# Latent attention: the queries' rotation done in the PSUM bank of their product, and both parts of all 96 rows made from it in one instruction each

## The chip, the cores and the metric

One core of a Trainium2 chip runs the whole program. The metric is the device time of one execution in microseconds, taken as the median of three runs. A profiled execution gives the rows shown below; L1561 is line 1561 of the kernel's file.

The engines are called PE or TensorE (matrix products), PEld (its weight loads), DVE or VectorE, ACT or ScalarE, POOL or GpSimd, and SP, which issues the DMAs. SBUF is the large on-chip memory, PSUM the one that TensorE writes to; PSUM has banks of 128 partitions by 512 fp32 columns. POOL's operands in this kernel are all in SBUF.

## The reference, cut to what matters

Two layers of a trunk over 256 context and 512 latent tokens. In each, a gated DeltaNet group and a latent attention group stand side by side, between two feed-forward parts. The attention has 8 heads with 64 plain dimensions and 32 rotated ones:

```python
q = (rmsnorm(c_q, q_norm) @ w_uq).reshape(B, T, 8, 64 + 32)
q_nope, q_rope = q[..., :64], q[..., 64:]
# latent tokens alone are rotated: x1*cos - x2*sin, x2*cos + x1*sin
q_rope = concatenate([q_rope[:, :L], rope2d(q_rope[:, L:], cos, sin)])
qf = concatenate([q_nope, q_rope], axis=-1)
kf = concatenate([k_nope, broadcast(k_rope)], axis=-1)
s = einsum('bqhd,bkhd->bhqk', qf, kf) * MLA_SCALE
p = softmax(s); o = einsum('bhqk,bkhd->bqhd', p, v)
```

Latent queries read all 768 keys, context queries the 256 of the context. In the second layer only latent queries are needed.

## The kernel before

Everything is kept with the channels on the partitions and the tokens along the columns. An fp32 operand is split into a high part (`h`, cast to fp32r) and the rest (`l`, the difference), and a product is made of three: high by high, high by low, low by high. So wherever a new operand arises, ScalarE makes the high part and VectorE or POOL subtracts it to make the low part.

`mla` does the attention of one layer, head by head. `prep(h)` lists what a head needs before its scores, in pieces:

- `q_proj` makes the queries' product in a PSUM bank named `qps` (9 matmuls of 512 columns for the latent tokens, 9 of 256 for the context). The weight columns are laid out so that rows 0 to 63 of the bank are the plain dimensions, 64 to 95 the rotated ones, and 96 to 127 the same with their halves exchanged. The table `tab` holds the cosines in rows 64 to 95 and the signed sines in rows 96 to 127, so a rotation is two products and a sum.
- `p_lat` makes `qh` and `ql`, the two parts of the latent queries: rows 0 to 63 plain, 64 to 95 rotated. This is the piece that the change edits. `p_ctx` does the same for the context's queries without a rotation, in the first layer alone.
- `p_keys` makes the keys' parts: for an even head from two products (`kps`), for an odd head from a copy `kp`.
- `p_max1` and `p_max2` multiply the high parts alone (`smx`, `smc`) and reduce each row's maximum on VectorE; `p_neg` and `p_row` turn it into one more row (row 96) of the queries, `rp`, so that the scores come out less the maximum.

Then come the scores of that head, `score` (`sT`: three matmuls of 512 columns for each tile of 128 keys, two exponentials on ScalarE to `ph` and to `pf` or `sum`, a difference `pl` at L1645 and a running sum at L1648), and three steps later `weigh` (`po`), and at a head's end the division (`dn`, `rb`, `oT`, L1670 to L1689). The pieces of head h+1 are dealt out among the score steps of head h. For heads 0 and 1 the pieces run ahead of all scores, and in the first of them the DeltaNet group's output norm (`out_norm`, L1398 to L1413, and L1424, L1425) still runs on the same engines.

PSUM's eight banks are divided for the attention: three (`mm0`) for `sT`, `vps`, `dn`, `rb`, `rp`; three (`mm1`) for `qps`, `smx`, `smc`, `kps`; two for `po` and others. A bank is given out again when all that use it are done. `qr` is a buffer of 128 by 1024 from the ring of four that the raw weights use too.

The order on each engine is not that of the text: a planner walks through the program with its own estimates of each instruction's time and of the priorities (`hp` raises one) and writes each engine's queue before the run. On the chip each queue runs strictly in that order and waits by semaphores.

Of the kernel before, what the change touches and what calls it, by code (L numbers as in the profile page):

```python
# [5 lines left out]
F32 = mybir.dt.float32  # L6
# [3 lines left out]
ALU = mybir.AluOpType  # L10
# [4 lines left out]
P = 128  # L15
NL = 512
# [18 lines left out]
class K:  # L35
# [1394 lines left out]
    def p3(self, ps, wh, wl, xs, kt, off, n, cnt):  # L1430
        nc = self.nc
        xh, xl = xs
        nc.tensor.matmul(ps, wh, xh[:, off : off + n], start=kt == 0, stop=False)
        nc.tensor.matmul(ps, wh, xl[:, off : off + n], start=False, stop=False)
        nc.tensor.matmul(ps, wl, xh[:, off : off + n], start=False, stop=kt == cnt - 1)
# [35 lines left out]
    def mla(self, l, last):  # L1471
        nc, d = self.nc, self.d
# [43 lines left out]
        n64, r32 = slice(0, 64), slice(64, 96)  # L1516

        def keys(pr):
            kh, kl = kb[0]
            kp = ap.tile([P, NT], F32, tag="kp", name="kp", bufs=1)  # L1520
            for off, n in ((0, NL), (NL, NC)):
                ps = self.kvp.pop(("k", pr, off), None) or self.k_prod(pr, off, n)
                c = slice(off, off + n)
                nc.scalar.copy(kh[n64, c], ps[n64])
                nc.vector.tensor_sub(kl[n64, c], ps[n64], kh[n64, c].bitcast(F32))
                nc.scalar.copy(kp[n64, c], ps[64:128])
            kpo[pr] = kp

        def prep(h):

            pr, odd = h // 2, h % 2
            kh, kl = kb[odd]
            qh, ql = qb[odd]
            mx = ap.tile([P, 8], F32, tag="mx", name="mx", bufs=2)
            m2 = ap.tile([P, 8], F32, tag="m2", name="m2", bufs=2)

            def q_proj(off, n):
                ps = self.bank("qps")[:, :n]
                for kt in range(3):
                    cs = slice((odd * 3 + kt) * P, (odd * 3 + kt + 1) * P)  # L1540
                    p3(ps, wq[pr][0][:, cs], wq[pr][1][:, cs], cq[kt], kt, off, n, 3)
                return ps

            def p_keys():
                if odd:
                    kp = kpo[pr]
                    (nc.scalar.copy if 0 else nc.vector.tensor_copy)(kh[n64, :], kp[n64, :])
                    (nc.vector if 0 else nc.gpsimd).tensor_sub(kl[n64, :], kp[n64, :], kh[n64, :].bitcast(F32))
                    if pr < 3:
                        wq[pr + 1] = self.load_w(d["uq"][l, pr + 1], 768)  # L1550
                else:
                    keys(pr)

            def p_lat():
                ps = q_proj(0, NL)
                c = slice(0, NL)
                t = self.wp.tile([P, 1024], F32, tag="raw", name="qr", bufs=4)
                u, w = t[:, 0:NL], t[:, NL : 2 * NL]
                nc.scalar.copy(u, ps)
                nc.scalar.copy(qh[n64, c], u[n64])  # L1560
                nc.vector.tensor_tensor(out=w[r32], in0=u[r32], in1=self.tab[r32], op=ALU.mult)  # L1561
                nc.vector.tensor_tensor(out=u[r32], in0=u[96:128], in1=self.tab[96:128], op=ALU.mult)  # L1562
                (nc.vector if 0 else nc.gpsimd).tensor_sub(ql[n64, c], u[n64], qh[n64, c].bitcast(F32))
                (nc.vector if 1 else nc.gpsimd).tensor_add(w[r32], w[r32], u[r32])
                nc.scalar.copy(qh[r32, c], w[r32])
                (nc.vector if 1 else nc.gpsimd).tensor_sub(ql[r32, c], w[r32], qh[r32, c].bitcast(F32))

            def p_ctx():
                if last:
                    return  # L1570
                ps = q_proj(NL, NC)
                c = slice(NL, NT)
                nc.scalar.copy(qh[0:96, c], ps[0:96])
                nc.vector.tensor_sub(ql[0:96, c], ps[0:96], qh[0:96, c].bitcast(F32))

            def p_max1(t):
                ps = self.bank("smx")
                nc.tensor.matmul(ps, qh[0:96, t * P : (t + 1) * P], kh[0:96, 0:NL], start=True, stop=True)
                nc.vector.reduce_max(mx[:, t : t + 1], ps, axis=AX)  # L1579

            def p_max2(t2):
                ps = self.bank("smc")
                for j in range(2):
                    t = 2 * t2 + j
                    nc.tensor.matmul(ps[:, j * 256 : (j + 1) * 256], qh[0:96, t * P : (t + 1) * P], kh[0:96, NL:NT], start=True, stop=True)
                nc.vector.reduce_max(m2[:, 2 * t2 : 2 * t2 + 2], ps.rearrange("p (a c) -> p a c", a=2), axis=AX)

            def p_neg():
                nc.vector.tensor_max(m2[:, 0:4], m2[:, 0:4], mx[:, 0:4])
                nc.vector.tensor_scalar(out=m2[:, :ntq], in0=m2[:, :ntq], scalar1=-1.0, scalar2=None, op0=ALU.mult)  # L1590

            def p_row():
                for g0, g1 in ((0, 4), (4, ntq)):
                    if g0 == g1:
                        continue
                    rp = self.bank("rp")
                    for t in range(g0, g1):
                        nc.tensor.matmul(rp[96:128, (t - g0) * P : (t - g0 + 1) * P], m2[:, t : t + 1].to_broadcast([P, 32]), self.ident, start=True, stop=True)
                    nc.scalar.copy(qh[96:97, g0 * P : g1 * P], rp[96:97, : (g1 - g0) * P])

            f = {}
            def at(i, p, *a, hi=0):
                def go():
                    with self.hp(hi and h > 0):
                        p(*a)
                f.setdefault(i, []).append(go)

            T = 91102222220 if last else 90112222333
            T = [int(c) for c in str(T)[1:]]
            if h < 2:  # L1610
                T = [1, 0, 2] + [3] * 7
            at(T[0], p_lat, hi=0)
            at(T[1], p_keys, hi=0)
            if not last:
                at(T[2], p_ctx, hi=0)
            for t in range(4):
                at(T[3 + t], p_max1, t, hi=1)
            for t in range(2 if last else 3):
                at(T[7 + t], p_max2, t, hi=1)
            at(max(T[3:10]), p_neg, hi=1)  # L1620
            at(6 if h < 2 else 5 if last else 6, p_row, hi=0)
            return [lambda i=i: [p() for p in f.get(i, [])] for i in range(8)]
# [78 lines left out]
        ps = prep(0)  # L1701
# [316 lines left out]
```

## Time and profile before

| | |
|---|---|
| median of 3 runs | 3298.61 us (3295.17 to 3299.12) |
| the profiled execution | 3296.14 us, span 3294.4 us |
| TensorE, VectorE, ScalarE, POOL busy | 93%, 77%, 42%, 39% of the span |
| granted clock of TensorE, mean | 0.953 of full speed |
| attention of the first layer | about 980 to 1155 us |
| attention of the second layer | about 2700 to 2870 us |

Busy shares are those of the whole span; the two attention stages take about a tenth of it. The span is the time from the first to the last instruction; the execution's own time is 1.7 us longer. An instruction's time in the profile includes what it waits inside the engine once it has started.

### The profile page before, as it was taken

The page shows a single profiled execution, that of the slowest core. Times are in us where ns is not written, and L with a number is a line of the kernel's source. Part 1 is how long each engine was busy: PE and PEld are TensorE (multiplying, and loading weights), DVE is VectorE, ACT ScalarE, POOL GpSimd, SP SyncE. Part 2 cuts the span into 40 slices and gives each one's busy share as a digit, 9 for nine tenths or more (in the row PEclk, how much of TensorE's full clock was granted, in tenths as well). Part 3 has the DMA queues.
Part 4 walks back from the last instruction along what each step waited for, and adds up shares of the span by engine and source line. Part 5 has one row for each costly group of instructions (what it writes and reads, how often), then busy time and mean ns, then how long its engine had stood idle before and what let it go on. Part 6 is the DMA issues. An engine that isn't in the chain of part 4 may idle for free. (4 is left out here: it accounts for less than half of the span.)

```text
span 3294.4 us, 53696 instructions
## 1 busy us (share of the span) xinstructions
PE 3056.4 (93%) x20836; PEld 2785.1 (85%) x20836; DVE 2550.1 (77%) x4369; ACT 1376.2 (42%) x2600; POOL 1298.7 (39%) x1028
## 2 busy tenths in 40 slices
PE   7999999889899999999999899999989788989998
PEld 4899989878787789899999898899877676789998
DVE  7788887777778958777777987677777879777777
ACT  4333223544445645322335432223454346554343
POOL 5222122544656664222215321221554546744233
PEclk8999999889998899999999899999989899999999
DMA  6333333221310122323324343332322310224333
GB/s 223 109 122 128 99 128 119 90 74 52 100 64 11 39 90 77 123 90 103 103 71 135 103 141 111 116 127 90 115 82 65 89 46 9 93 77 154 97 109 97
DMA packets 149815, 318.68 MB, mean 97 GB/s; under 512 B 38184, under 2 KB 79528, under 8 KB 149560
## 3 DMA queue, kind: packets, MB, share of 16 engines
q1 hardware_dynamic: 149560, 315.25, 29.4%
q8 instruction: 163, 2.67, 0.3%
q14 instruction: 92, 0.75, 0.1%
HBM read 285.17 MB, written 30.03 MB: 96 GB/s over the span
## 5 line engine op out<-in xcount | busy, mean ns | idle before, releaser
L94 POOL TENSOR_TENSOR wlo<-wraw,whi 128x1024 fp32r<-128x1024 f32 (+1 forms) x228 | 589.6, 2596 | 1396.5 <-ACT whi L93 1357.5
L93 ACT CAST whi<-wraw 128x1024 fp32r<-128x1024 f32 (+2 forms) x482 | 469.4, 978 | 712.5 <-PE ps L778 344.8
L519 PE MATMUL ps<-zh,whi 128*128 128x256 f32 (+1 forms) x1208 | 386.1, 328 | 8.8 <-ACT zh L472 8.8
L609 PE MATMUL ps<-zl,whi 128*128 128x384 f32 (+1 forms) x1216 | 391.8, 322 | 0.0
L608 PE MATMUL ps<-zh,whi 128*128 128x384 f32 (+1 forms) x1216 | 391.6, 322 | 0.1
L610 PE MATMUL ps<-zh,wlo 128*128 128x384 f32 (+1 forms) x1216 | 390.3, 321 | 0.0
L520 PE MATMUL ps<-zl,whi 128*128 128x256 f32 (+1 forms) x1208 | 378.6, 324 | 5.7 <-DVE zl L477 5.7
L777 PE MATMUL ps<-gh,whi 128*128 128x512 f32 (+1 forms) x1008 | 350.6, 356 | 17.7 <-ACT gh L618 16.7
L778 PE MATMUL ps<-gl,whi 128*128 128x512 f32 (+1 forms) x1008 | 341.4, 354 | 25.4 <-DVE gl L619 25.4
L522 PE MATMUL ps<-zh,wlo 128*128 128x256 f32 (+1 forms) x1208 | 350.1, 323 | 0.1
L94 DVE TENSOR_TENSOR wlo<-wraw,whi 128x1024 fp32r<-128x1024 f32 (+1 forms) x254 | 295.3, 1163 | 24.8 <-ACT whi L93 23.4
L780 PE MATMUL ps<-gh,wlo 128*128 128x512 f32 (+1 forms) x1008 | 297.9, 350 | 0.0
L519 PEld LDWEIGHTS ps<-zh,whi 128*128 128x128 f32 x1208 | 234.5, 198 | 38.5 <-ACT zh L472 11.2
L520 PEld LDWEIGHTS ps<-zl,whi 128*128 128x128 f32 x1208 | 236.4, 196 | 24.2 <-DVE zl L477 6.6
L777 PEld LDWEIGHTS ps<-gh,whi 128*128 128x128 f32 x1008 | 193.4, 194 | 61.8 <-ACT gh L618 19.5
L778 PEld LDWEIGHTS ps<-gl,whi 128*128 128x128 f32 x1008 | 194.6, 193 | 54.9 <-DVE gl L619 27.9
L243 DVE CUSTOM_DVE_ANT_0 abraw<-abraw,srow 128x1024 f32<-128x1024 f32 x128 | 210.2, 1642 | 32.1 <-DMA abraw<-in_wat 29.9
L608 PEld LDWEIGHTS ps<-zh,whi 128*128 128x128 f32 x1216 | 229.4, 189 | 1.8 <-ACT whi L93 0.5
L609 PEld LDWEIGHTS ps<-zl,whi 128*128 128x128 f32 x1216 | 229.5, 189 | 0.4
L610 PEld LDWEIGHTS ps<-zh,wlo 128*128 128x128 f32 x1216 | 229.0, 188 | 0.0
L522 PEld LDWEIGHTS ps<-zh,wlo 128*128 128x128 f32 x1208 | 221.0, 197 | 6.9 <-issue 0.7
L608 PE MATMUL ps<-t42h,whi 128*128 128x384 f32 (+1 forms) x608 | 197.3, 324 | 7.6 <-ACT whi L93 7.6
(394 smaller groups left out, 7615.2 us busy)
## 6 DMA issues: line engine op xcount, KB each, us to landing
wraw<-in_wu SPq DMA_DIRECT2D x176, 512.0 KB, 3.3
abraw<-in_wat SPq DMA_DIRECT2D x128, 512.0 KB, 3.4
wraw<-in_wd SPq DMA_DIRECT2D x88, 512.0 KB, 3.5
wraw<-in_wi SPq DMA_DIRECT2D x44, 512.0 KB, 3.4
wraw<-in_wo SPq DMA_DIRECT2D x16, 512.0 KB, 3.8
xs<-x SPq DMA_DIRECT2D x64, 128.0 KB, 1.7
x<-xs SPq DMA_DIRECT2D x64, 128.0 KB, 3.3
x<-in_x SPq DMA_DIRECT2D x48, 128.0 KB, 3.5
```

Of the source, the lines that this page charges most:

```text
L93: nc.scalar.copy(hi[:, :n], raw[:, :n])
L94: (eng or nc.gpsimd).tensor_sub(lo[:, :n], raw[:, :n], hi[:, :n].bitcast(F32))
L243: self.nc.vector.tensor_tensor_reduce(out=dst, in0=w, in1=self.srow[:, v, a:b], scale=1.0, scalar=start, op0=ALU.mult, op1=ALU.add, accum_ ...
L519: nc.tensor.matmul(ps, wh, self.zh[k][:, off : off + n], start=first, stop=False)
L520: nc.tensor.matmul(ps, wh, self.zl[k][:, off : off + n], start=False, stop=False)
L522: nc.tensor.matmul(ps, wl, self.zh[k][:, off : off + n], start=False, stop=last)
L608: nc.tensor.matmul(ps, w[0][:, c], xh, start=k == 0, stop=False)
L609: nc.tensor.matmul(ps, w[0][:, c], xl, start=False, stop=False)
L610: nc.tensor.matmul(ps, w[1][:, c], xh, start=False, stop=k == 3)
L777: nc.tensor.matmul(ps, wh[:, o : o + P], gh[j][:, off : off + n], start=j == 0, stop=False)
L778: nc.tensor.matmul(ps, wh[:, o : o + P], gl[j][:, off : off + n], start=False, stop=False)
L780: nc.tensor.matmul(ps, wl[:, o : o + P], gh[j][:, off : off + n], start=False, stop=j == nf - 1)
```

## The change

`p_lat` alone is changed. Before, ScalarE copies the whole bank to SBUF (`u`), and the work goes on from that copy: a cast of rows 0 to 63 and POOL's difference for them, two products with the table, a sum, a cast of rows 64 to 95 and VectorE's difference. After, VectorE reads the bank itself: it multiplies rows 96 to 127 into a buffer, multiplies rows 64 to 95 in place in the bank, adds the buffer to them there; then one cast of rows 0 to 95 by ScalarE and one difference of rows 0 to 95 by VectorE make both parts. Per head ScalarE has one instruction in place of three, POOL none in place of one, VectorE four in place of four.

```diff
             def p_lat():
                 ps = q_proj(0, NL)
                 c = slice(0, NL)
-                t = self.wp.tile([P, 1024], F32, tag="raw", name="qr", bufs=4)
-                u, w = t[:, 0:NL], t[:, NL : 2 * NL]
-                nc.scalar.copy(u, ps)
-                nc.scalar.copy(qh[n64, c], u[n64])
-                nc.vector.tensor_tensor(out=w[r32], in0=u[r32], in1=self.tab[r32], op=ALU.mult)
-                nc.vector.tensor_tensor(out=u[r32], in0=u[96:128], in1=self.tab[96:128], op=ALU.mult)
-                (nc.vector if 0 else nc.gpsimd).tensor_sub(ql[n64, c], u[n64], qh[n64, c].bitcast(F32))
-                (nc.vector if 1 else nc.gpsimd).tensor_add(w[r32], w[r32], u[r32])
-                nc.scalar.copy(qh[r32, c], w[r32])
-                (nc.vector if 1 else nc.gpsimd).tensor_sub(ql[r32, c], w[r32], qh[r32, c].bitcast(F32))
+
+                u = self.wp.tile([P, 1024], F32, tag="raw", name="qr", bufs=4)[:, 0:NL]
+                nc.vector.tensor_tensor(out=u[r32], in0=ps[96:128], in1=self.tab[96:128], op=ALU.mult)
+                nc.vector.tensor_tensor(out=ps[r32], in0=ps[r32], in1=self.tab[r32], op=ALU.mult)
+                nc.vector.tensor_add(ps[r32], ps[r32], u[r32])
+                nc.scalar.copy(qh[0:96, c], ps[0:96])
+                nc.vector.tensor_sub(ql[0:96, c], ps[0:96], qh[0:96, c].bitcast(F32))
```

## Rows read from the trace of the kernel before

**Rows 1.** By stage: us; PE, PEld, DVE, ACT, POOL busy (instructions); clock; DMA.

```profile
1010.00:1150.00 140.00, 130.24 (x683) 103.02 (x681) 126.53 (x179) 88.72 (x180) 93.95 (x64) 0.90 0.08 26
2700.00:2740.00 40.00, 30.81 (x135) 22.54 (x133) 36.11 (x52) 22.03 (x43) 23.31 (x15) 0.87 0.03 10
2740.00:2840.00 100.00, 87.72 (x431) 67.14 (x430) 97.56 (x117) 61.20 (x112) 72.34 (x47) 0.93 0.09 27
...
2760.00:2780.00 20.00, 20.00 (x113) 16.19 (x112) 18.89 (x30) 12.79 (x27) 11.22 (x8) 0.98 0.07 20
```

**Rows 2.** Waits from 2740 to 2840 us: total, times, longest.

```profile
PEld po L1664 <- DVE pl L1645: 7.8, 7, 3.4
...
PE sT L1632 <- DVE oT L1686: 5.6, 3, 2.3
```

**Rows 3.** The chain that ended last, 2690 to 2870 us: start, us, what.

```profile
by line: DVE pl L1645 13.4%; DVE mx L1579 6.6%; issue 6.5%; DVE qr L1562 4.2%; DVE qr L1561 3.8%; DVE m L1586 3.3%; PE sT L1632 3.2%; DVE wlo L94 2.6%; DVE qr L1564 2.6%; PE sT L1634 2.5%; PE sT L1633 2.4%; PE smx L1578 2.2%; PE po L1663 2.
...
2709.45 0.86 DVE g L1566
...
2837.27 0.68 DVE qbl L1566
```

**Rows 4.** Groups of the rotation, whole span: busy us, mean ns; idle before.

```profile
L1564 DVE TENSOR_TENSOR qr<-qr 32x512 f32<-32x512 f32 x16 | 22.0, 1376 | 0.5
L1562 DVE TENSOR_TENSOR qr<-qr,tab 32x512 f32<-32x512 f32 x16 | 16.5, 1030 | 0.5
L1561 DVE TENSOR_TENSOR qr<-qr,tab 32x512 f32<-32x512 f32 x16 | 15.9, 994 | 5.3 <-ACT qr L1559 4.9
L1566 DVE TENSOR_TENSOR qbl<-qr,qbh 32x512 fp32r<-32x512 f32 x8 | 9.8, 1219 | 0.3
L1566 DVE TENSOR_TENSOR g<-qr,g 32x512 fp32r<-32x512 f32 x8 | 8.1, 1011 | 0.4 <-ACT g L1565 0.2
...
L1563 POOL TENSOR_TENSOR g<-qr,g 64x512 fp32r<-64x512 f32 x8 | 13.2, 1650 | 0.0
```

**Rows 5.** Instructions on `qr`: duration ns min/median/max, first and last start us.

```profile
L1559 ACT COPY qr<-qps x16: 562/587/589, 981.4 to 2827.3; 128x512 f32<-128x512 f32 x16
L1561 DVE TENSOR_TENSOR qr<-qr,tab x16: 682/707/2176, 983.5 to 2829.5; 32x512 f32<-32x512 f32 x16
...
L1560 ACT CAST g<-qr x8: 606/620/623, 982.0 to 2808.4; 64x512 fp32r<-64x512 f32 x8
```

**Rows 6.** Timeline of one head, 2807 to 2812 us: start, us, engine.

```profile
2808.32 1.67 DVE L1561 TENSOR_TENSOR qr<-qr,tab 32x512 f32<-32x512 f32 x1
2810.02 1.64 DVE L1562 TENSOR_TENSOR qr<-qr,tab 32x512 f32<-32x512 f32 x1
...
2807.21 0.59 ACT L1559 COPY qr<-qps 128x512 f32<-128x512 f32 x1 [1.69 <-PE qps L1435]
...
2809.40 1.70 POOL L1563 TENSOR_TENSOR g<-qr,g 64x512 fp32r<-64x512 f32 x1
```

**Rows 7.** Groups of VectorE without and with PSUM operands, whole span.

```profile
L1645 DVE TENSOR_TENSOR pl<-pf,ph 128x512 fp32r<-128x512 f32 x66 | 80.0, 1217 | 7.3 <-ACT pf L1644 6.3 <-PE dn L1679 0.3
...
L617 DVE TENSOR_TENSOR ps<-ps,c 128x384 f32<-128x384 f32 x57 | 31.8, 559 | 0.9
...
L630 DVE TENSOR_TENSOR u<-p,ps 128x384 f32<-128x384 f32 x57 | 31.2, 548 | 14.2 <-PE ps L610 14.0
...
L1525 DVE TENSOR_TENSOR g<-kps,g 64x512 fp32r<-64x512 f32 x8 | 5.4, 678 | 0.1
```

**Rows 8.** Timeline of the first layer's start, VectorE and TensorE.

```profile
987.45 3.40 DVE L1564 TENSOR_TENSOR qr<-qr 32x512 f32<-32x512 f32 x1
...
987.57 1.09 PE L1411 MATMUL otp<-cm,o 128*128 128x128 f32 x4 [5.51 <-DVE o L1406]
991.55 1.22 PE L1578 MATMUL smx<-g,g 96*128 96x512 f32 x2 [2.90 <-ACT g L1565]
```

**Rows 9.** Tile `smx`: idle before it (us, times), by what ended it.

```profile
  ACT kp L1526: 3.1, 6
```

## Prediction

> **What bounds the kernel now.** I read the page's busy times first (the table above). Over the whole span TensorE is the busiest engine, at 93%, and VectorE has 77%. That average says nothing about a change of sixteen short passages, so I went to the table by stage for the two attention stages [rows 1]. There the picture turns. From 2740 to 2840 us, well inside the second layer's attention, VectorE is busy 97.56 of 100 us, that is, it rests 2.4 us; TensorE is busy 87.72 and rests 12.3. In the first layer's steady part, 1010 to 1150 us, VectorE has 126.53 of 140 and TensorE 130.24: two engines close to full, neither alone in charge. At the second layer's start (2700 to 2740) TensorE lies idle 9.2 us of 40, and VectorE is again the fuller one, with 36.11.
>
> Next the waits of that 100 us window [rows 2]. What TensorE waits for is VectorE: 7.8 us before the weight load for `po`, for `pl` (L1645), and 5.6 us before `sT` for `oT` (L1686). Weight loads and products overlap, so the two aren't added; the reader is to see that the name behind the arrow is VectorE each time. Last, the chain that ended last, in the stretch 2690 to 2870 [rows 3]. The rotation's own lines stand on it: L1562 with 4.2%, L1561 with 3.8% and L1564 with 2.6% of these 180 us, which is 7.6, 6.8 and 4.7 us in 5, 5 and 4 pieces; L1566 adds four pieces, the first and last of which are shown, 4.3 us together. So 23.4 us of the second layer's chain are instructions of the edited function. The chain isn't followed back into the first layer, so that stage is judged from [rows 1] alone.
>
> **The change part by part.** VectorE has four instructions per head before and after, 16 heads in the two layers. Before [rows 4]: 15.9 + 16.5 + 22.0 + 9.8 + 8.1 = 72.3 us, 4.5 us a head, though the shortest L1561 takes 0.68 us [rows 5]. Why they are longer is seen in a head of the second layer [rows 6]: L1561 and L1562 take 1.67 and 1.64 us, and beside them POOL runs L1563, 1.70 us, between two runs of L1648. All of these have both inputs in SBUF, and each of VectorE's is as long as one of POOL's: the two engines take turns.
>
> After the change all four have one input in PSUM. The trace has that kind [rows 7]: the keys' difference (L1525), 64 rows by 512, PSUM and SBUF in, takes 0.678 us in the mean, the eight together 5.4. In the same stage, beside the same POOL, L1645 with both inputs in SBUF takes 1.217 in the mean. The write into PSUM is shown too: L617 writes `ps` from `ps` in place and takes 0.559 us for 384 columns, L630 writes the same size to SBUF in 0.548. So I take 0.69 us each, 2.76 a head, 44.2 us for 64: 28.1 us less of VectorE, 14 in each layer. Bounds: nothing saved, if two PSUM sides at 512 columns cost what L1564 does now (1.376, 88 us for 64, then even 16 us lost); at best 0.678, 28.9 saved. I take the value near the low end, for the rows with a PSUM input have it and the other is a row without one. The 96 rows in place of 32 I cost at nothing: L1525 with 64 rows and the shortest L1561 with 32 are the same 0.68.
>
> [...]
>
> ScalarE loses the copy (0.587), one cast of 64 rows (0.62) and one of 32, and gains one cast of 96 rows; I take all three casts at 0.62, for the copy of 128 rows is no longer than that: 1.2 us a head, 19 us less in all [rows 5]. It is busy 61.20 of 100 us in the window [rows 1], so this is worth nothing by itself; it is covered by VectorE, and if that cover went it could be worth a part of a us per head where its casts stand ahead of the exponentials. The cast of 96 rows waits for VectorE's sum, as L1565 did before, and behind it on ScalarE's queue stand the exponentials of the head before, for which TensorE's `po` waits; that wait is not new, and it should be shorter.
>
> POOL loses L1563, of which eight are shown with 13.2 us and the other eight have the same: 26.4 us [rows 4]. POOL isn't the bound (72.34 of 100 us [rows 1]). But each of these runs is one that VectorE can collide with. Bounds: nothing, or all of 1.65 - 0.68, about 1 us a head, 8 a layer. I take 2 us a layer, as most of VectorE's other instructions there read PSUM (`smx`, `smc`, `oT`).
>
> The way from the product to `qh` loses one ScalarE step and a hand-over. At the first layer's start [rows 8] L1564 alone takes 3.40 us beside POOL, so that `smx` starts at 991.55, after two rests of TensorE of 5.51 and 2.90 us. Instructions of the output norm (L1413, L1406) stand between the rotation's, and they stay. I take off the excess of L1564, 2.7 us, and nothing for the earlier start, since the norm's steps come next in any case: about 3 us in the first layer; what there is in the second is in its chain already.
>
> No DMA is added or removed, and the `qr` buffer stays, so SP's queue sees at most an earlier release.
>
> **Sum.** Second layer: on the chain, 18 pieces at 0.69 are 12.4 us in place of 23.4, so 11.0; plus 2 for POOL. Not all comes out, as TensorE needs its own time: at the rate of 2760 to 2780 (113 matmuls in 20 us, the one slice where it never rests [rows 1]) the 431 matmuls of the 100 us window need 76 us, so there is room for 24, but VectorE rested 2.4 us and other waits fill in: I take 10, the start included. First layer: VectorE saves 14 too, but it rests 13.5 of 140 us and TensorE only 9.8. I take 4 in the steady part, and 3 at the start: 7. Together 17 us. From the profiled execution's 3296.1 that is 3279; that execution lies 2.5 below the median of the three runs, 3298.6, so against it 3282 would be the same saving. I say **3280**.
>
> **Rivals.**
> 1. *Saved on VectorE, not on the clock.* Each engine's order is written by the planner before the run. If another wait is last behind each removed one (ScalarE's exponentials, the row of maxima), of the 17 us only the first start comes out, 3 us, or nothing: 3293 to 3299 by the two bases. For it: in the first layer TensorE is fuller than VectorE [rows 1]. Against it: the chain of [rows 3].
> 2. *The bank, slower.* The product's bank was free after ScalarE's copy; now it is held until the last subtraction. `qps`, `kps` (two banks), `smx` and `smc` share three banks. In the head of [rows 6] the copy L1559 ended at 2807.8, while a sum of three times 0.69, a cast and a subtraction at 0.69 from 2808.3 gives 2812 without any queueing, some 4 us later, and the maxima's products need those banks. TensorE already waits there 3.1 us in 6 cases for the copies that free `kps` [rows 9]. If each head waits on it for two more subtractions' length with hand-over, 1.5 to 2 us, 16 heads lose 24 to 32 us, less the 17: 3303 to 3314 by the two bases. It decides from 17/16, about 1.1 us a head. Against it: the first `smx` can't run before the cast anyway, and only one VectorE instruction lies between the cast and the release. [...] In this trace the copies that free `kps` late cost only those 3.1 us.
> 3. *Another order.* With other instructions and costs the planner may write a different order in and behind the attention. One that puts the maxima a place too early or late costs or gains a VectorE instruction per head, 16 x 0.68 = 11 us either way around the forecast: 3269 to 3291.
>
> **Chances.** Forecast 0.55 (3272 to 3290); order 0.15, split about evenly to both sides, all of it still below 3292; rival 1 0.16; rival 2 0.14. What a measurement tells from no change here is 0.2%, 6.6 us, so faster is under 3292.0 and slower over 3305.2. Faster: 0.55 + 0.15 = 0.70, less 0.02 for a mix of order and bank, 0.68; slower: most of rival 2, 0.12; the rest, 0.20, is the same. The range leaves out the upper part of rival 2 and the lowest orders: 3267 to 3302. The forecast's own is 3272 to 3290.
>
> **What would show it.** VectorE's four groups of the rotation at 0.68 to 0.70 us each with no spread, some 44 us together; POOL without its 26 us; VectorE's rests in the middle of the second layer above 2.4 us or that stage about 10 us shorter; L1645's mean under 1.217. Against it would speak waits of `smx` or `kps` for the subtraction above 1 us a head, waits for `pl` as long as before, or 64-instruction sums above 60 us. Wrong altogether it would be if the stages are shorter and the rest longer, for then the order behind them has changed.

## The result and the profile after

The changed kernel takes **3272.88 us** (median of 4 runs, 3270.34 to 3276.36) against 3296.89 for the kernel before in the same set of runs: a ratio of 0.9929 [0.9916, 0.9941], 24.0 us or 0.7% faster. A second set (below) gives 0.9923; where a kernel of another set is held against the changed one, I take the middle of the two, 0.9926 of that set's time before, 24.4 us less. The profiled execution spans 3270.0 us, 24.4 less than the one before, at a mean granted clock of 0.959 (before 0.953).

The page's busy times, changed kernel:

```profile
PE 3039.8 (93%) x20836; PEld 2775.2 (85%) x20836; DVE 2520.6 (77%) x4369; ACT 1354.1 (41%) x2568; POOL 1265.7 (39%) x1012
```

VectorE has 29.5 us less than before, ScalarE 22.1, POOL 33.0. TensorE has the same instructions and is still busy 16.6 us less; where that comes from is seen below. The groups of the rotation, changed kernel (busy us, mean ns; idle before it), which answer to [rows 4], and below them the cast (its instructions: ns min/median/max, first and last start):

```profile
L1561 DVE TENSOR_TENSOR qps<-qps,qr 32x512 f32<-32x512 f32 x16 | 11.2, 703 | 0.5
L1560 DVE TENSOR_TENSOR qps<-qps,tab 32x512 f32<-32x512 f32 x16 | 11.2, 703 | 0.5
L1559 DVE TENSOR_TENSOR qr<-qps,tab 32x512 f32<-32x512 f32 x16 | 11.1, 695 | 3.4 <-PE qps L1435 3.1
L1563 DVE TENSOR_TENSOR g<-qps,g 96x512 fp32r<-96x512 f32 x8 | 5.4, 679 | 0.1
L1563 DVE TENSOR_TENSOR qbl<-qps,qbh 96x512 fp32r<-96x512 f32 x8 | 5.4, 678 | 1.2 <-ACT qbh L1562 1.1
```

```profile
L1562 ACT CAST g<-qps x8: 581/582/600, 986.7 to 2792.7; 96x512 fp32r<-96x512 f32 x8
```

The sum over the 64 instructions is 44.3 us, where [rows 4] held 72.3. The table by stage, changed kernel: the window of the first layer lies 10 us earlier than in [rows 1], as all work does there, and the windows of the second layer are cut so that they hold the same TensorE work (434 matmuls where the 100 us window of [rows 1] holds 431):

```profile
1000.00:1140.00 140.00, 133.53 (x736) 107.17 (x737) 126.89 (x192) 86.82 (x180) 88.37 (x62) 0.96 0.13 37
2690.00:2727.00 37.00, 31.18 (x126) 24.34 (x127) 28.94 (x49) 18.02 (x37) 15.19 (x10) 0.79 0.04 11
2727.00:2820.00 93.00, 84.71 (x434) 66.67 (x433) 85.29 (x116) 56.09 (x102) 59.77 (x39) 0.94 0.13 39
```

About as many matmuls take 93 us in place of 100, and VectorE, which rested 2.4 us of that window, rests 7.7. In the first layer 736 matmuls pass in 140 us in place of 683, and the clock there is 0.96 in place of 0.90.

Where the 24.4 us come off, measured from a stage's first product of `qps` to the stores of `x` behind it (the first of them for the first layer, the last for the second): 1.0 us before the first attention stage; the first stage takes 226.5 us in place of 239.7, so 13.2; between the stages 1.7; the second stage takes 232.4 in place of 240.9, so 8.5; behind it nothing.

Not all waits went. The waits of 2727 to 2820 us, changed kernel (total us, times, longest), answer to [rows 2]:

```profile
PEld po L1661 <- DVE pl L1642: 8.8, 6, 4.8
```

and the group of that `pl`, changed kernel, to the first row of [rows 7]:

```profile
L1642 DVE TENSOR_TENSOR pl<-pf,ph 128x512 fp32r<-128x512 f32 x66 | 82.9, 1262 | 8.6 <-ACT pf L1641 7.4 <-PE sT L1631 0.7
```

TensorE waits for `pl` as long as before, and `pl` itself got a little longer (1.262 us in the mean, before 1.217). The chain that ended last, changed kernel, 2680 to 2850 us, answers to [rows 3]:

```profile
by line: DVE pl L1642 15.4%; issue 7.7%; DVE mx L1576 5.0%; POOL sum L1645 3.5%; PE sT L1629 3.3%; DVE m L1586 3.3%; PE sT L1631 3.2%; PE sT L1630 3.1%; PE po L1661 2.5%; DVE qps L1560 2.5%; PE smx L1575 2.5%; DVE m L1583 2.5%; PE rb L1682 
```

Of the rotation's lines, 4.2, 3.8 and 2.6% before, L1560 stands there with 2.5% and no other is among the twelve that the row gives in full; `pl` leads.

### The profile page after: what moved, and what is told of

The parts are those of the page before. It is cut to its first block, busy times and chain, and to the rows that moved or that the text cites. A ratio compares the mean times of both kernels' runs of the same rounds, so it can differ in the third digit from the quotient of the medians.

```text
span 3270.0 us, 53665 instructions
## 1 busy us (share of the span) xinstructions
PE 3039.8 (93%) x20836; PEld 2775.2 (85%) x20836; DVE 2520.6 (77%) x4369; ACT 1354.1 (41%) x2568; POOL 1265.7 (39%) x1012
## 5 line engine op out<-in xcount | busy, mean ns | idle before, releaser
L94 POOL TENSOR_TENSOR wlo<-wraw,whi 128x1024 fp32r<-128x1024 f32 (+1 forms) x228 | 591.1, 2604 | 1396.9 <-ACT whi L93 1357.8
L94 DVE TENSOR_TENSOR wlo<-wraw,whi 128x1024 fp32r<-128x1024 f32 (+1 forms) x254 | 293.4, 1155 | 29.5 <-ACT whi L93 28.0
```

Source lines behind the costliest of these rows:

```text
L94: (eng or nc.gpsimd).tensor_sub(lo[:, :n], raw[:, :n], hi[:, :n].bitcast(F32))
```

## The experiments

My theory at the start: the time came out of VectorE, because its instructions no longer have both inputs in SBUF and so no longer take turns with POOL. Rivals: that POOL's (or ScalarE's) removed work did it, that the shorter way to `qh` did it, that the bank held longer gives some of it back, and that the order which the planner writes carries part of the difference. The experiments were run in three sets, each on one chip with its own runs of the kernel before (medians 3292.78, 3299.94 and 3299.93), so ratios are compared.

**The rotation alone** is made from the bank; the plain rows 0 to 63 go the old way, over ScalarE's copy, ScalarE's cast and POOL's difference.

```diff
-                nc.scalar.copy(u, ps)
+                nc.scalar.copy(u[n64], ps[n64])
...
+                nc.vector.tensor_tensor(out=u[r32], in0=ps[96:128], in1=self.tab[96:128], op=ALU.mult)
+                nc.vector.tensor_tensor(out=ps[r32], in0=ps[r32], in1=self.tab[r32], op=ALU.mult)
+                nc.vector.tensor_add(ps[r32], ps[r32], u[r32])
...
+                nc.scalar.copy(qh[r32, c], ps[r32])
+                nc.vector.tensor_sub(ql[r32, c], ps[r32], qh[r32, c].bitcast(F32))
```

> The rotation is read from the bank as in the change (three VectorE instructions and a difference of rows 64 to 95, all with a PSUM input), but the plain rows 0 to 63 go the old way: ScalarE copies and casts them, POOL subtracts. My theory, that the gain is VectorE no longer taking turns with POOL in these four instructions: they stay at 0.68 to 0.70 us, some 44 us in all, and 16 to 20 of the 24 us stay, the rest lost to POOL's 16 differences. Rival, that POOL's and ScalarE's removed work is the gain: within 5 us of the kernel before. Rival, that the planner's new order is the gain: anything between 0 and 30 us faster, with VectorE's sum unrelated to it.

Measured: 3274.53 us, 0.9939 [0.9926, 0.9952]. Of 24.4 us 18 (by the medians) to 20 (by the ratio) stay, with POOL's sixteen differences still there (25.0 us, of which eight are the first row) and VectorE's at their short durations (one of its groups is the second row; groups as above):

```profile
L1565 POOL TENSOR_TENSOR qbl<-qr,qbh 64x512 fp32r<-64x512 f32 x8 | 13.3, 1662 | 11.8 <-issue 11.6 <-ACT qbh L1561 0.2
...
L1564 DVE TENSOR_TENSOR qps<-qps,qr 32x512 f32<-32x512 f32 x16 | 11.3, 703 | 0.5
```

So three quarters of the gain or more come with the rotation's operands; the interval reaches the changed kernel's 0.9926. The shorter way to `qh` isn't priced by itself: the first product sits idle 3.8 us for ScalarE's copy here, and 4.9 in the kernel before [rows 4].

**The plain rows alone** come from the bank, cast by ScalarE and subtracted by VectorE; the rotation stays in SBUF.

```diff
-                nc.scalar.copy(u, ps)
-                nc.scalar.copy(qh[n64, c], u[n64])
+                nc.scalar.copy(u[64:128], ps[64:128])
+                nc.scalar.copy(qh[n64, c], ps[n64])
...
-                (nc.vector if 0 else nc.gpsimd).tensor_sub(ql[n64, c], u[n64], qh[n64, c].bitcast(F32))
+                nc.vector.tensor_sub(ql[n64, c], ps[n64], qh[n64, c].bitcast(F32))
```

> The other part alone: the plain rows are cast and subtracted straight from the bank (POOL's difference goes, VectorE has one more instruction with a PSUM input), while the rotation works from ScalarE's copy in SBUF as before. My theory: VectorE's three instructions with two SBUF inputs stay near 1.0 to 1.4 us each, the fifth adds 16 x 0.68 = 11 us, so between 2 us faster and 8 us slower than before. Rival, that POOL's removed work is the gain: 10 us or more faster.

Measured: 3288.26 us, 0.9984 [0.9975, 0.9993], 4.5 us faster than before, more than the 2 that I had allowed and less than the rival's 10. POOL's work is gone here, and the rotation is only a little shorter; its sum and one of its products in this kernel (groups):

```profile
L1565 DVE TENSOR_TENSOR qr<-qr 32x512 f32<-32x512 f32 x16 | 20.3, 1270 | 0.5
...
L1562 DVE TENSOR_TENSOR qr<-qr,tab 32x512 f32<-32x512 f32 x16 | 16.7, 1041 | 4.4 <-ACT qr L1560 4.0
```

Other POOL work stands beside them: with POOL's sixteen taken away the sum still takes 1.270 us in the mean, before 1.376. The two halves, 18 to 20 and 4.5 us, about make the 24.4, though the order moved in each.

**The bank held.** To the kernel before, a read of one column of the bank is added behind the last difference, so that the bank comes free as late as in the changed kernel.

```diff
+                nc.vector.tensor_tensor(out=w[r32, 0:1], in0=ps[r32, 0:1], in1=ql[r32, 0:1].bitcast(F32), op=ALU.mult)
```

> The kernel before with one thing added: after the last difference VectorE reads one column of the product's bank (32 rows by 1, about 0.1 to 0.2 us), so that the bank is held as long as in the change, with all else as before. My theory, that the hold is nearly free: 16 x 0.15 = 2.4 us and a little waiting, 0 to 6 us slower than before. Rival, that the hold has a price which the change pays too and hides behind its gain: 10 us or more slower, with waits of smx or qps for VectorE's last instruction in the trace.

Measured: 3292.9 us, 0.9999 [0.9990, 1.0008]; the read takes 0.156 us each time (instructions on `qr`, this kernel: min/median/max ns):

```profile
L1567 DVE TENSOR_TENSOR qr<-qps,g x8: 156/156/156, 990.7 to 2811.1; 32x1 f32<-32x1 f32 x8
```

The 24 to 32 us of that rival aren't there. The bank isn't free of waits: products of `smx` wait 2.9 us in 5 cases for the added read, and in the changed kernel 4.3 us in 4 for its last difference. The order moved here too, and the four instructions of the rotation took 65.5 us in place of 72.3, so a price of a few us can hide behind that.

**A fifth product.** To the changed kernel one more VectorE instruction per head is added, of the kind that it has, into a spare buffer.

```diff
+                nc.vector.tensor_tensor(out=w[r32], in0=ps[96:128], in1=self.tab[96:128], op=ALU.mult)
```

> The changed kernel with the first product made a second time into a spare place: one more VectorE instruction per head, with a PSUM input, 0.70 us, 11.1 us in all. It prices VectorE's time. My theory, that VectorE sets the pace of both attention stages and TensorE's clock adds to it: 8 to 14 us slower than the changed kernel, that is 10 to 16 us faster than before. Rival, that VectorE now has room and only the collisions mattered: within 3 us of the changed kernel, 21 to 27 us faster than before.

Measured: 3258.73 us, 0.9898 [0.9881, 0.9914]: some 10 us *faster* than the changed kernel, with 11 us more of VectorE. This is a miss that no theory of work explains. The fifth product changes what the planner sees, and its order with it. In this order `pl` is shorter (group, this kernel):

```profile
L1644 DVE TENSOR_TENSOR pl<-pf,ph 128x512 fp32r<-128x512 f32 x66 | 72.6, 1103 | 10.0 <-ACT pf L1643 9.7
```

72.6 us in place of 82.9, so the shorter `pl` nearly gave back the added 11 us. The stages take 224.9 and 228.9 us (changed kernel 226.5 and 232.4), and the work between them, which no edit touches, 3.5 us less. What makes this order better beyond `pl` I can't say from these runs.

**The changed kernel again**, in the second set, without an edit:

> The changed kernel once more, on the same chip as the three below, so that differences of less than 10 us between kernels of its family can be read. Both theories: 3268 to 3278 us.

Measured: 3272.58 us, 0.9923 [0.9905, 0.9942]. The result repeats.

**POOL's work back.** To the changed kernel a difference of 64 rows is added on POOL, into a spare buffer; it reads the cast.

```diff
+                nc.gpsimd.tensor_sub(w[n64], self.tab[n64], qh[n64, c].bitcast(F32))
```

> The changed kernel with POOL's difference of 64 rows put back as spare work (both inputs in SBUF, 16 times 1.3 to 1.7 us), written to a place that nothing reads. It prices POOL's part alone. My theory, that POOL collides with VectorE's other instructions with two SBUF inputs, about 2 us a layer: 2 to 8 us slower than the changed kernel. Rival, that the order which the planner writes moves the time by as much: anything from 8 us faster to 8 us slower, with the sum of VectorE's L1645 kind rising all the same.

Measured: 3285.7 us, 0.9959 [0.9947, 0.9972], 13 us slower than the changed kernel in the same set. But the group shows what was added with it (this kernel; the last column is idle time ahead of it):

```profile
L1565 POOL TENSOR_TENSOR qr<-tab,qbh 64x512 f32<-64x512 f32 x8 | 11.7, 1464 | 19.0 <-ACT qbh L1563 19.0
```

POOL's whole queue stood behind the cast for 19.0 us (and 7.1 in the other eight). So this prices a wait on POOL as well as its work, and was repeated without the wait:

```diff
+                nc.gpsimd.tensor_sub(w[n64], self.tab[n64], self.tab[n64])
```

> The changed kernel with 16 spare differences of 64 rows by 512 on POOL that wait for nothing but a free buffer and are read by nothing (both inputs are the table). It mends the earlier run, in which POOL's spare work waited for ScalarE's cast and its queue stood behind it. Theory of the turns, that VectorE's two-SBUF instructions and POOL's share one resource which is the tightest one in the stage: 16 x 1.27 = 20 us more of it, 8 to 20 us slower than the changed kernel. Theory of VectorE's time, that only VectorE's own instructions count: 0 to 5 us slower. Theory of POOL's queue, that the 13 us of the earlier run were its wait for the cast: 0 to 5 us slower as well.

Measured: 3279.8 us, 0.9943 [0.9931, 0.9956], about 4 us slower than the changed kernel, but the intervals overlap. The group, this kernel, waits for nothing:

```profile
L1565 POOL TENSOR_TENSOR qr<-tab 64x512 f32<-64x512 f32 x16 | 17.7, 1106 | 0.1
```

The engines' orders are nearly those of the changed kernel (112 of 16197 TensorE entries, like matmuls in a row counted as one, stand in another place). But this is less than the work that was removed: two of the sixteen run ahead of the stages (at 936 and 2649 us), and together they run beside VectorE's instructions with two SBUF inputs for 4.5 us, where L1563 of the kernel before did so for 20.0, 13.1 of them beside the rotation itself. What the removed POOL work was worth stays open; about 4 us is what this run gives, not told apart from nothing.

**The sum from SBUF.** In the changed kernel the second product goes to SBUF, so that one instruction of four has both inputs there again.

```diff
-                nc.vector.tensor_tensor(out=ps[r32], in0=ps[r32], in1=self.tab[r32], op=ALU.mult)
-                nc.vector.tensor_add(ps[r32], ps[r32], u[r32])
+                nc.vector.tensor_tensor(out=w[r32], in0=ps[r32], in1=self.tab[r32], op=ALU.mult)
+                nc.vector.tensor_add(ps[r32], w[r32], u[r32])
```

> The changed kernel with the second product written to SBUF, so that the sum has both inputs in SBUF and writes the bank. One instruction in four gets two SBUF inputs again, nothing else changes. My theory, that two SBUF inputs are what lengthens: this sum has a mean of 1.0 to 1.5 us in place of 0.703 and a spread up to 3 us, the other three stay at 0.70, 5 to 12 us of VectorE come back, and the kernel is 3 to 10 us slower than the changed one. Rival, that SBUF or PSUM makes no difference and the copy by ScalarE did: the sum stays at 0.70 and so does the kernel.

Measured: 3269.69 us, 0.9915 [0.9897, 0.9933], no difference from the changed kernel that these intervals show. The sum did get longer, less than expected (instructions on `qr`, this kernel: min/median/max ns):

```profile
L1562 DVE TENSOR_TENSOR qps<-qr x16: 671/698/1766, 984.0 to 2798.0; 32x512 f32<-32x512 f32 x16
```

Half of the sixteen took 0.698 us or less, as if alone; the mean is 0.935 us, so 3.7 us more in all. The effect sought was too small for a kernel whose order also moved.

**The products swapped**: the same instructions, the second product written ahead of the first.

```diff
-                nc.vector.tensor_tensor(out=u[r32], in0=ps[96:128], in1=self.tab[96:128], op=ALU.mult)
                 nc.vector.tensor_tensor(out=ps[r32], in0=ps[r32], in1=self.tab[r32], op=ALU.mult)
+                nc.vector.tensor_tensor(out=u[r32], in0=ps[96:128], in1=self.tab[96:128], op=ALU.mult)
```

> The changed kernel with the two products in the other order: the same instructions, the same inputs, only the text's order differs, and with it perhaps what the planner writes. It prices the order alone. Theory, that the order is worth several us either way, as the fifth product suggests, which made the kernel faster: 4 to 15 us apart from the changed kernel, with VectorE's sum of the rotation at 44 us as before. Rival, that the order is worth nothing: within 3 us.

Measured: 3276.48 us (3264.73 to 3287.06), 0.9934 [0.9911, 0.9957], within the changed kernel's interval, with 254 of 16197 TensorE entries in another place.

So far each edit moved the order too. The next two don't differ in it.

**Spare products, from PSUM and from SBUF.** Both kernels add four VectorE products per head to the changed kernel, into a spare buffer. In the first all four read the bank; in the second three of the four read both inputs from SBUF.

The line that the first has four times:

```diff
+                nc.vector.tensor_tensor(out=w[r32], in0=ps[r32], in1=ql[r32, c].bitcast(F32), op=ALU.mult)
```

and the one that the second has three times, ahead of one of the first:

```diff
+                nc.vector.tensor_tensor(out=w[r32], in0=u[r32], in1=ql[r32, c].bitcast(F32), op=ALU.mult)
```

> The changed kernel with four spare VectorE products per head behind the last difference, 32 rows by 512, one input in PSUM, read by nothing: 64 x 0.68 = 43.5 us more of VectorE. Theory of VectorE's time, that it sets the pace as the prediction had it: 30 to 40 us slower than the changed kernel. Theory of the turns, that a third of VectorE's busy time is waiting for POOL and that work from PSUM falls into it: 5 to 20 us slower.

> The same as the run before it in this list, with the same order of instructions on every engine, but three of the four spare products have both inputs in SBUF (the fourth reads the bank as before). Theory of VectorE's time: the same within 5 us, as all four have the same shortest time. Theory of the turns: 48 x 0.68 = 33 us more of the shared resource, 15 to 35 us slower than with the inputs in PSUM, the spare products from SBUF at 1.0 us or more in the mean and those from PSUM at 0.69.

Measured: from PSUM 3313.55 us, 1.0048 [1.0036, 1.0061]; from SBUF 3325.86 us, 1.0082 [1.0069, 1.0096], on the same chip. The two stand in the same order on VectorE, ScalarE and POOL, instruction by instruction, and on TensorE but for four matmuls at 876 us, ahead of both stages (two profiles of the changed kernel itself differ in eight); only the inputs of 48 differ. Two groups of the first kernel, with the others like them:

```profile
L1567 DVE TENSOR_TENSOR qr<-qps,qbl 32x512 f32<-32x512 f32 x8 | 5.5, 689 | 0.3
...
L1565 DVE TENSOR_TENSOR qr<-qps,g 32x512 f32<-32x512 f32 x8 | 5.5, 690 | 0.3
```

The six groups of the second:

```profile
L1567 DVE TENSOR_TENSOR qr<-qr,qbl 32x512 f32<-32x512 f32 x8 | 10.4, 1296 | 0.3
L1566 DVE TENSOR_TENSOR qr<-qr,qbl 32x512 f32<-32x512 f32 x8 | 9.0, 1121 | 0.3
L1565 DVE TENSOR_TENSOR qr<-qr,qbl 32x512 f32<-32x512 f32 x8 | 8.0, 999 | 0.3
L1566 DVE TENSOR_TENSOR qr<-qr,g 32x512 f32<-32x512 f32 x8 | 6.4, 795 | 0.3
L1565 DVE TENSOR_TENSOR qr<-qr,g 32x512 f32<-32x512 f32 x8 | 5.9, 743 | 0.3
L1567 DVE TENSOR_TENSOR qr<-qr,g 32x512 f32<-32x512 f32 x8 | 5.5, 683 | 0.3
```

Two things follow. From the first kernel: 64 more instructions of 0.689 us are 44 us of VectorE and cost 38 us of the whole (3313.55 less 0.9926 of 3299.93), 0.86 for one, a change of order included; the theory of VectorE's time had 30 to 40, that of the turns 5 to 20. So in these stages nearly all of VectorE's added time, 38 of 44 us, came out as the kernel's. From the pair: the six groups take 45.2 us where the same 48 took 33.1 from PSUM, 12.1 more on VectorE, and the kernel is 12.3 us longer; 11.4 of the 11.8 us between the profiled executions lie in the two stages. That is less than the 15 to 35 us of the theory of the turns and more than the 5 of the theory of VectorE's time. With order, count and work equal, the place of the inputs alone costs 0.26 us of the whole per instruction.

That they are long where POOL runs beside them, the two traces show as well. A long and a short one of the second kernel, and what POOL ran at that time (timeline):

```profile
2820.84 2.31 DVE L1565 TENSOR_TENSOR qr<-qr,qbl 32x512 f32<-32x512 f32 x1
2824.51 0.68 DVE L1566 TENSOR_TENSOR qr<-qr,qbl 32x512 f32<-32x512 f32 x1
...
2820.77 1.84 POOL L94 TENSOR_TENSOR wlo<-wraw,whi 128x768 fp32r<-128x768 f32 x1
2822.57 1.72 POOL L1691 TENSOR_TENSOR zl<-oT,zh 64x512 fp32r<-64x512 f32 x1
```

Of the 48 from SBUF, 22 have no POOL instruction beside them and take 0.682 to 0.685 us each; the other 26 take 0.682 to 2.308, 1.156 in the mean. The same 48 from PSUM take 0.689 to 0.692, though 27 of them stand beside POOL. The kernel before is the same: of the rotation's 64 instructions, 19 without POOL took 0.682 to 0.689, 45 beside it 1.317 in the mean.

So the same 48 take 0.940 us in the mean with two SBUF inputs, and 0.689, almost without spread, with one.

**The head outputs too.** In the changed kernel the same edit is made for the outputs' normalization: the product in place in the bank `rb`, cast and difference from there by ScalarE and VectorE; POOL's 24 differences go, and VectorE gets 14 us more.

```diff
-                nc.vector.tensor_tensor(out=o[ob], in0=ps[n64, :n], in1=o[n64], op=ALU.mult)
+                nc.vector.tensor_tensor(out=ps[ob, :n], in0=ps[ob, :n], in1=o[ob], op=ALU.mult)
...
-                nc.scalar.copy(oh, o[ob])
-                nc.gpsimd.tensor_sub(self.zl[4 + pr][ob, off : off + n], o[ob], oh.bitcast(F32))
+                nc.scalar.copy(oh, ps[ob, :n])
+                nc.vector.tensor_sub(self.zl[4 + pr][ob, off : off + n], ps[ob, :n], oh.bitcast(F32))
```

> A version that should beat both: the changed kernel, and the same change made to the heads' outputs. The division's product is written in place in its PSUM bank, ScalarE casts it from there, and VectorE makes the low part from there; POOL's 24 differences (L1686, 29.5 us in the two layers) go, VectorE has 24 more instructions with a PSUM input (16 x 0.68 + 8 x 0.41 = 14 us). Theory of the turns: 8 to 20 us faster than the changed kernel. Theory of VectorE's time: 5 to 14 us slower. Rival, that the banks of the scores are missed, since the output's bank is held longer: slower, with waits of sT for VectorE's difference.

Measured: 3271.15 us, 0.9912 [0.9899, 0.9926], about 4 us better than the changed kernel and not told apart from it, short of the 8 to 20 that the turns gave. VectorE's new differences and the `pl` of this kernel (groups):

```profile
L1642 DVE TENSOR_TENSOR pl<-pf,ph 128x512 fp32r<-128x512 f32 x66 | 71.7, 1090 | 6.9 <-ACT pf L1641 5.6 <-PE sT L1631 0.9
...
L1686 DVE TENSOR_TENSOR zl<-rb,zh 64x512 fp32r<-64x512 f32 x16 | 11.0, 685 | 1.1 <-ACT zh L1685 0.9
```

With POOL's work away `pl` gives back 11.2 us, about what the added instructions take: moving work from POOL to VectorE about paid for itself here, with an order that moved too.

## Why the prediction was right, point by point

**VectorE's durations: right.** 44.2 us were forecast for the 64 instructions, 44.3 measured, all between 0.670 and 0.704 us. The upper bound, 1.376 us for a sum with two PSUM sides, has no place: such a sum takes 0.703.

**Cause: right.** That two SBUF inputs beside POOL make these instructions longer, and the kernel with them, is shown by the pair of spare products (0.940 us in the mean for 0.689, the kernel 12.3 us longer); that it is most of this change's gain, by the rotation alone, with an order that moved too. Estimates for the change: 64 instructions at the pair's 0.26 us are 16 us; one for one, the 28.0 us that VectorE's 64 lost would be 28. The 18 to 20 us of the rotation alone lie between. What the new order adds to the 24.4 or takes from it, no run separates.

**The sum: right, in part by luck.** 17 us were forecast and 24 came off, at the very edge of the forecast's own 3272 to 3290. The order, which the fifth product puts at some 20 us, could have carried the time out of it.

**POOL: open.** 2 us a layer were forecast; the spare differences came out at about 4 in all, which is not told apart from nothing and stands for less POOL work than was removed. The expectation that went with it, `pl` under 1.217 us, is **wrong**: 1.262. POOL has fewer instructions, but `pl` meets them no less: 62 of its 66 stood beside one before and 61 do after, and 38 in place of 34 take over 1 us. `pl` has both inputs in SBUF and is VectorE's largest group in the window of [rows 1], which my reason for the small figure, that most of the others read PSUM, left out.

**ScalarE: right.** 19 us less forecast, 22.1 measured; the cast of 96 rows 0.582 us, not 0.62. Nothing shows that it was worth time.

**The start of the first layer: right.** The first row of maxima (`rp`) starts at 998.30 us in place of 1002.24; 1.0 of these 3.9 came before the stage, so 3, as forecast.

**The first layer's steady part: mis-sized, the step that failed.** I took 4 us because TensorE "rests only 9.8" of 140 us. The stage gave 13.2 in all, 3 at the start and so 10 behind it. TensorE's rests were no ceiling, because its *busy* time held time at the lower clock, and [rows 1] said so: 0.90 in that window, which with the two levels that the windows below show, 0.50 and 1.00, is a fifth of the 140 us at the lower one, an estimate; now it is 0.96. One head has most of it. From its row of maxima to the next, it took 28.1 us (1087.89 to 1115.96) and takes 20.1 (1080.24 to 1100.38), 8 of the 10 us; in the second profile of the changed kernel it takes 20.2. The timeline of that head, kernel before: `pl` on VectorE, what POOL ran beside it, and TensorE's next step with its rest in brackets:

```profile
1089.52 3.06 DVE L1645 TENSOR_TENSOR pl<-pf,ph 128x512 fp32r<-128x512 f32 x1
...
1088.56 1.71 POOL L1563 TENSOR_TENSOR qbl<-qr,qbh 64x512 fp32r<-64x512 f32 x1
1090.23 1.79 POOL L94 TENSOR_TENSOR wlo<-wraw,whi 128x768 fp32r<-128x768 f32 x1
...
1092.63 0.69 PE L1664 MATMUL po<-pl,vb 128*64 128x512 f32 x1 [2.36 <-DVE pl L1645]
```

The windows behind it, kernel before (columns as in [rows 1]):

```profile
1093.00:1104.00 11.00, 11.00 (x36) 9.15 (x36) 9.11 (x15) 5.12 (x11) 5.01 (x5) 0.50 0.28 97
1104.00:1116.00 12.00, 12.00 (x64) 9.02 (x63) 9.80 (x15) 7.16 (x14) 9.34 (x7) 0.95 0.00 0
1088.00:1116.00 28.00, 24.94 (x110) 19.58 (x110) 23.84 (x32) 14.70 (x31) 19.36 (x14) 0.76 0.11 38
```

The same head in the changed kernel, `pl` and POOL in the timeline and the window:

```profile
1080.20 1.31 DVE L1642 TENSOR_TENSOR pl<-pf,ph 128x512 fp32r<-128x512 f32 x1
...
1080.92 2.27 POOL L94 TENSOR_TENSOR wlo<-wraw,whi 128x768 fp32r<-128x768 f32 x1
```

```profile
1080.00:1100.00 20.00, 19.31 (x109) 15.10 (x108) 19.77 (x29) 11.33 (x25) 17.19 (x12) 1.00 0.18 54
```

Before, `pl` took 3.06 us beside two POOL instructions, one of them the removed L1563; TensorE rested 2.36 us for it, and in the 11 us that follow it is busy without a gap at a clock of 0.50: 36 matmuls in 11 us, then 64 in 12. After, the same head's `pl` takes 1.31 us, and 109 matmuls pass in 20 us at 1.00. So more than the rest's 2.36 us was lost here. That the low level came from this rest was not tried by itself; the clock stands at 1.00 up to 1091 us and at 0.50 from 1092, within the rest. Nor is it the removed L1563 alone: that ended at 1090.27, and `pl` went on beside L94, which stays. After, the two meet again, and there it is L94 that takes longer, 2.27 us for 1.79, so part of these 8 us hangs on which of the two came first.

**The second layer: right.** 10 us forecast, 8.5 measured, and 1.0 and 1.7 us came off outside the stages, which I had left at nothing. One sign that I had named against the change came all the same: TensorE waits for `pl` as long as before, 8.8 us for 7.8.

**Rival 1, saved on VectorE alone: fell.** It gave 3 us or nothing.

**Rival 2, the bank: fell** at its price of 24 to 32 us, by the held bank and by the changed kernel's own 4.3 us of waits.

**Rival 3, the order: real, and priced too low.** I gave it 11 us either way. The fifth product is 10 us faster with 11 us more work; at the 0.86 of the spare products it should have been 10 slower, so its order is worth some 20, an estimate.

**"VectorE is the fuller one": half right.** VectorE's busy 97.56 of 100 us held time above what the same instructions take at their shortest. With each of the 117 instructions of that window at the shortest duration of its line and shape in this trace, VectorE has 67.7 us of work; the 53 with two SBUF inputs take 66.0 us there and would take 33.2 (one instruction's record overlaps the next's a little, so the differences don't add up to the busy time exactly). So about a third of what I read as work was lengthening. In the changed kernel's 93 us 34 such instructions are left, with 41.8 us for 21.2. Nor did POOL and these instructions fill the window between them: in 12.4 of the 100 us neither POOL nor an instruction with two SBUF inputs ran.

## What to carry to other kernels

Where VectorE and POOL work side by side, read the spread of VectorE's durations before its busy share: an instruction whose mean is well above its shortest, with both inputs in SBUF, may be lengthened by POOL: here the rotation's without POOL beside them were all at the shortest (0.682 to 0.689 us, those beside it 1.317 in the mean), and with one operand left in the PSUM bank where the product made it they took 0.670 to 0.704. When a stage's gain is bounded by what TensorE rests, add what it loses at a lower clock behind the rests, where the windows show one (here 11 us at 0.50 behind a rest of 2.36). And with a planner's order a single edit can move the order by as much as its own worth or more, so test a cause on two kernels whose orders are the same.

## What the runs showed of the hardware

- VectorE's spare products with two SBUF inputs were longer only with a POOL instruction beside them: 22 of 48 without one took 0.682 to 0.685 us, 26 with one up to 2.308; with one input in PSUM all took 0.689 to 0.692.
- An in-place product or sum in PSUM with 32 rows of 512 took 0.703 us, PSUM to SBUF 0.689 to 0.695, and the shortest from SBUF 0.682: operands in PSUM cost 1 to 3% here, whereas two SBUF inputs beside POOL up to doubled the mean ([rows 4], 1.376).
- 96 rows took about what fewer did: 0.678 us for the difference (32 rows in the rotation alone 0.689), 0.582 for ScalarE's cast from the bank (32 rows in the rotation alone 0.577; its cast of 64 rows from SBUF took 0.620 [rows 5]).
- One collision was long: `pl` at 3.06 us is 2.4 us above what L1525 needs for as many columns [rows 7], as two POOL instructions, L1563 and L94, ran one after the other beside it.
